# An encoder block's head: which channel blocks share a bank of the transposes, and where VectorE's second copy of weights stands

## The chip, the cores and the metric

The kernel runs on one core of a Trainium2 chip. The metric is the device time of one execution, in microseconds, as the median of several runs. Beside it there is one profiled execution, whose trace gives a start and a duration for each instruction. The engines are named as in the profile: PE is TensorE (PEld its weight loads), ACT is ScalarE, DVE is VectorE, POOL is GpSimd, SP is SyncE, which issues most of the loads.

## What is computed

One layer of an encoder block on 256 tokens of 1024 channels, in float32:

```
h  = RMSNorm(x)                       # 256 x 1024
z  = h @ W_in                         # pool-in, pool-gate, q, k, v, attn-gate, merge gates
yA = (pooled(z.pool_in) * silu(z.pool_gate)) @ W_a
yB = (dilated_attention(q, k, v) * silu(z.attn_gate)) @ W_b
y  = RMSNorm(x + (sigmoid(gA) * yA + sigmoid(gB) * yB) @ W_out)
```

The attention has three groups of eight heads with windows of different dilation, combined by their softmax denominators. The matrix products must keep nearly the accuracy of float32.

## The kernel before

**Products in three passes.** An operand a is split into a high part, a rounded to the format float32r, and a low part, the rest. A product is then three matmuls into one accumulator: high by high, high by low, low by high. For the weights the parts are called `whi` and `wlo`, for the normalised and transposed tokens `hh` and `hl`. The weights come in pieces of about 1 MB in a fixed order (`wraw0`, `wraw1`, ...), four buffers deep; ACT makes `whi` (line 128) and DVE makes `wlo` (line 133) of a piece, in halves, while PE still works on earlier pieces.

**The head.** Everything that the change touches stands in the first part of `encoder_block`, which is written under a manual schedule: ACT, DVE, PE and POOL execute it in the order of the text, and waits are set where an instruction needs another engine's result. Two engines that access one PSUM bank are given such a wait too. In order:

- PE multiplies a dummy tile while the tokens load. The tokens `X` come in two halves of 128 tokens (b = 0, 1).
- For each half, ACT and DVE sum the squares of one half of the channels each, POOL makes the reciprocal root `rs`, and DVE (line 194, channels 0 to 511) and ACT (line 195, channels 512 to 1023) scale it to `XN`.
- DVE rounds piece 0 of the weights to `whi` in two copies of 128 x 1024 (line 197), each when its half of the load has landed. POOL then makes `wlo` of it in two subtractions (lines 199 and 200, helper at line 163).
- PE transposes `XN` in sixteen steps of 128 x 128 (`turn`, line 204): eight channel blocks kc for b = 0, then for b = 1. The transposed blocks lie in four PSUM banks `tp0` to `tp3` of two blocks each. Block kc lies in bank kc % 4, so blocks 0 and 4 share a bank, 1 and 5, and so on. For b = 1 the order of the transposes is 0, 4, 1, 5, 2, 6, 3, 7, which completes one bank after the other.
- For each kc, ACT reads the block from its bank, multiplies it by the norm's gain and rounds it to `hh` (line 223); DVE reads the same block, multiplies it likewise and subtracts `hh`, which gives `hl` (line 224).
- PE multiplies the blocks with piece 0 of the weights as they come (`part0`, line 213): the pair of matmuls (for the two column blocks) with `hh` of block kc, then the pair with `hl` of block kc - 2; at the end the two last pairs with `hl`. After these 32 matmuls come 16 with `wlo` and `hh`, of which the last six, for blocks 5 to 7, need POOL's second subtraction. Before these six stand a few small matmuls for the position bias (line 237).

After the head PE goes on with piece 1 of the weights (`project_t`, lines 247 to 249 in `mm3`), and so on through all pieces, with the attention's steps in between.

Of the kernel before, what the change touches and what calls it, by code (L numbers as in the profile page):

```python
# [17 lines left out]
P = 128  # L18
# [24 lines left out]
def encoder_block(ctx: ExitStack, tc: tile.TileContext, x, w_in, lines, w_pool, w_proj_a, w_proj_b,  # L43
                  w_out, final_gain, params, out):
    nc = tc.nc
# [7 lines left out]
    def slot(shape, dt, tag, name, bufs=1):  # L53
        return sb.tile(shape, dt, tag=tag, name=name, bufs=bufs)
# [6 lines left out]
    def bank(shape, tag, name, bufs):  # L61
        return ps.tile(shape, F32, tag=tag, name=name, bufs=bufs)
# [8 lines left out]
    ident = sb.tile([P, P], F32, name="ident")  # L71
# [64 lines left out]
    def cut_next():  # L136
        cut_half()
        cut_half()
# [16 lines left out]
    XN = slot([P, 2, D], F32, "v", "XN", 2)  # L155
# [5 lines left out]
    def cut_lo(n, k0, k1, eng):  # L161
        t, (hi, lo) = raws[n][0], parts[n]
        return eng.tensor_tensor(lo[:, k0:k1, :], t[:, k0:k1, :], hi[:, k0:k1, :].bitcast(F32), op=ALU.subtract)

    def open_parts(n):
        shp = raws[n][1]
        parts[n] = (slot([P] + shp, F32R, "whi", f"whi{n}", 3), slot([P] + shp, F32R, "wlo", f"wlo{n}", 3))
        state["cut"] = 2 * n + 2

    with tc.manual_schedule(engines={mybir.EngineType.Activation, mybir.EngineType.DVE, mybir.EngineType.PE,  # L170
                                    mybir.EngineType.Pool}):
        tiny = sb.tile([P, 1], F32, name="tiny")
        warm = sb.tile([P, P], F32, name="warm")
        nc.vector.memset(warm, 0.0)
        nc.scalar.activation(tiny, warm[:, 0:1], AF.Square)

        def keep_warm(times):
            for _ in range(times):
                nc.tensor.matmul(misc[:, P:2 * P], warm, warm, start=True, stop=True)

        keep_warm(WARM)
        halves = [slice(h * 512, (h + 1) * 512) for h in range(2)]
        for b in range(2):
            sq = [slot([P, 512], F32, "st", f"sq{b}{h}", 3) for h in range(2)]
            nc.scalar.activation(sq[0], X[:, b, halves[0]], AF.Square, scale=1.0 / 32.0, accum_out=ss[:, b, 0:1])
            xb = X[:, b, halves[1]]
            nc.vector.tensor_tensor_reduce(sq[1], xb, xb, scale=1.0 / D, scalar=EPS, op0=ALU.mult, op1=ALU.add,
                                           accum_out=ss[:, b, 1:2])
            t = slot([P, 1], F32, "rt", f"rt{b}", 2)
            nc.vector.tensor_tensor(t, ss[:, b, 0:1], ss[:, b, 1:2], op=ALU.add)  # L190
            nc.gpsimd.tensor_tensor(rs[:, b:b + 1], t, mhalf, op=ALU.pow)
        open_parts(0)
        for b in range(2):
            nc.vector.tensor_scalar(XN[:, b, halves[0]], X[:, b, halves[0]], rs[:, b:b + 1], None, op0=ALU.mult)
            nc.scalar.activation(XN[:, b, halves[1]], X[:, b, halves[1]], AF.Copy, scale=rs[:, b:b + 1])
        for k in (0, 4):
            nc.vector.tensor_copy(parts[0][0][:, k:k + 4, :], raws[0][0][:, k:k + 4, :])

        cut_lo(0, 0, 5, nc.gpsimd)
        first_lo = cut_lo(0, 5, 8, nc.gpsimd)  # L200
        tps = [bank([P, 2, S], "mm" if i < 3 else "T", f"tp{i}", 3 if i < 3 else 2) for i in range(4)]

        def turn(kc, b):
            nc.tensor.transpose(tps[kc % 4][:, kc // 4, b * P:(b + 1) * P], XN[:, b, kc * P:(kc + 1) * P], ident)

        acc = bank([P, 2, 512], "S", "k00", 1)
        acc0 = [acc[:, u, 0:S] for u in range(2)]

        def part0(kc, x):
            hi_, lo_ = parts[0]  # L210
            for u in range(2):
                c = slice(u * P, (u + 1) * P)
                nc.tensor.matmul(acc0[u], (lo_ if x == 2 else hi_)[:, kc, c], (hl if x == 1 else hh)[:, kc, :],
                                 start=x == 0 and kc == 0, stop=x == 2 and kc == KC - 1)

        for kc in range(KC):
            turn(kc, 0)
        for kc in range(KC):
            turn(kc // 2 + kc % 2 * 4, 1)
        for kc in range(KC):  # L220
            v = tps[kc % 4][:, kc // 4]
            gcol = prm[:, kc:kc + 1]
            nc.scalar.activation(hh[:, kc, :], v, AF.Copy, scale=gcol)
            nc.vector.scalar_tensor_tensor(hl[:, kc, :], v, gcol, hh[:, kc, :].bitcast(F32), op0=ALU.mult,
                                           op1=ALU.subtract)
            part0(kc, 0)
            if kc >= 2:
                part0(kc - 2, 1)
        for kc in (6, 7):
            part0(kc, 1)  # L230
        for kc in range(KC):
            if kc == 5:

                for t in range(3):
                    w = 3 * NH
                    o = 3 * P + t // 2 * w
                    nc.tensor.matmul(misc[:, t * w:(t + 1) * w], oh[:, t * P:(t + 1) * P], oh[:, o:o + w],
                                     start=True, stop=True)
            part0(kc, 2)
        cut_next()  # L240
        nc.vector.tensor_copy(line.rearrange("p i r h -> p r i h"),
                              misc[:, 0:LROW * NH].rearrange("p (r i h) -> p r i h", i=2, h=4))
        cut_next()
# [270 lines left out]
    for g, w in enumerate(POOL_W):  # L514
        h = w // 2
        cur, lo_, n_ = U[:, g, :], 0, UW
        k = 1
# [305 lines left out]
```

## Time and profile before

| | us |
|---|---|
| median of 3 runs (lowest to highest) | 260.86 (260.79 to 261.13) |
| the profiled execution, its own time | 260.82 |
| its span, from the first instruction's start to the last one's end | 259.0 |
| PE busy | 250.4 |
| DVE busy | 210.2 |
| ACT busy | 164.4 |
| POOL busy | 74.5 |

In rows of the timeline the first number is the start in us from the beginning of the span, the second the duration in us. Then come the engine, the line of the code, the operation, the tiles written and read, their shapes and the count of instructions that the row holds. In brackets stands how long the engine was idle before, and what ended that. A row whose count is over 1 holds neighbours of the same kind, of which one may begin before the last has ended. Ends of matmuls are modelled, so their starts are the better measure.

### The profile page before, as it was taken

What the parts mean: (1) busy time and instruction counts of PE and PEld (TensorE: products, weight loads), DVE (VectorE), ACT (ScalarE), POOL (GpSimd) and SP (SyncE); (2) the same over time, 40 slices, a digit from 0 to 9 for tenths busy, and PEclk for the clock granted to TensorE, in tenths of its full rate; (3) what the DMA queues carried; (4) which work ended last, traced back from release to release, by engine and by line L of the source; (5) the groups of instructions that cost most, each with busy time, mean ns of one, the idle gap of its engine ahead of it and who ended that gap; (6) DMA issues with size and microseconds to landing.
All of it is one profiled execution on the core that took longest, in us unless ns stands there. A gap on an engine that the chain in (4) does not pass through costs nothing.

```text
span 259.0 us, 5482 instructions
## 1 busy us (share of the span) xinstructions
PE 250.4 (97%) x2160; PEld 248.8 (96%) x2160; DVE 210.2 (81%) x412; ACT 164.4 (63%) x285; POOL 74.5 (29%) x101
## 2 busy tenths in 40 slices
PE   7899999999999999999999999999999999999990
PEld 7899999999999999999999999999999999999990
DVE  2899988778888787889697997967859988899383
ACT  4878577565666565658967777765457797446141
POOL 1563386002798000010763910000010020442011
PEclk9999999999999999999999999999999999999998
DMA  6999999984445553444989867144440696300022
GB/s 231 393 412 363 239 323 329 313 306 162 166 162 172 235 172 156 162 164 162 284 254 257 278 216 273 47 164 162 164 162 6 209 383 233 148 4 0 0 84 81
DMA packets 9992, 52.01 MB, mean 201 GB/s; under 512 B 1147, under 2 KB 2142, under 8 KB 4718
## 3 DMA queue, kind: packets, MB, share of 16 engines
q1 hardware_dynamic: 7022, 44.08, 48.4%
q0 software_dynamic: 2512, 7.12, 11.1%
q10 hardware_dynamic: 432, 0.46, 0.5%
q8 instruction: 17, 0.28, 0.4%
q14 instruction: 9, 0.07, 0.1%
HBM read 47.42 MB, written 1.09 MB: 187 GB/s over the span
## 4 chain that ended last, share of the span: by engine, by line
PE 84%; DVE 6%; issue 3%; ACT 2%; DMA 2%; POOLq 0%; POOL 0%; SPq 0%; DVEq 0%; ACTq 0%
PE v L249 4%; PE v L248 4%; PE q L249 4%; PE q L248 4%; PE v L247 4%; PE q L247 4%; PE g L247 4%; PE g L248 4%; PE g L249 4%; PE k L247 4%; PE k L249 4%; PE k L248 4%; PE y L247 2%; PE y L248 2%; PE y L249 2%
## 5 line engine op out<-in xcount | busy, mean ns | idle before, releaser
L133 DVE TENSOR_TENSOR wlo<-wraw,whi 128x512 fp32r<-128x512 f32 (+2 forms) x134 | 108.5, 849 | 8.3 <-ACT whi L128 7.3
L128 ACT ACTIVATE whi<-wraw 128x1024 fp32r<-128x1024 f32 (+1 forms) x80 | 81.0, 1038 | 23.2 <-PE q L248 10.1
L247 PE MATMUL g<-hh,whi 128*128 128x256 f32 x128 | 35.8, 280 | 0.0
L249 PE MATMUL g<-hh,wlo 128*128 128x256 f32 x128 | 35.4, 277 | 0.0
L248 PE MATMUL g<-hl,whi 128*128 128x256 f32 x128 | 35.4, 276 | 0.0
L304 ACT ACTIVATE st<-st,nm 128x512 f32<-128x512 f32 x16 | 11.6, 722 | 29.6 <-DVE nm L301 29.6
L247 PE MATMUL v<-whi,hh 128*128 128x256 f32 x96 | 26.6, 277 | 0.0
L249 PE MATMUL v<-whi,hl 128*128 128x256 f32 x96 | 26.5, 276 | 0.0
L248 PE MATMUL v<-wlo,hh 128*128 128x256 f32 x96 | 26.5, 276 | 0.0
L249 PE MATMUL q<-hh,wlo 128*128 128x256 f32 x96 | 26.5, 276 | 0.0
L247 PE MATMUL q<-hh,whi 128*128 128x256 f32 x96 | 26.5, 276 | 0.0
L248 PE MATMUL q<-hl,whi 128*128 128x256 f32 x96 | 26.5, 276 | 0.0
L247 PEld LDWEIGHTS g<-hh,whi 128*128 128x128 f32 x128 | 24.0, 188 | 0.1
L248 PEld LDWEIGHTS g<-hl,whi 128*128 128x128 f32 x128 | 24.1, 188 | 0.0
L249 PEld LDWEIGHTS g<-hh,wlo 128*128 128x128 f32 x128 | 24.0, 188 | 0.0
L247 PE MATMUL k<-hh,whi 128*128 128x256 f32 x80 | 22.2, 277 | 0.0
L249 PE MATMUL k<-hh,wlo 128*128 128x256 f32 x80 | 22.1, 277 | 0.0
L248 PE MATMUL k<-hl,whi 128*128 128x256 f32 x80 | 22.1, 277 | 0.0
L248 PEld LDWEIGHTS v<-wlo,hh 128*128 128x128 f32 x96 | 18.0, 188 | 0.0
L249 PEld LDWEIGHTS q<-hh,wlo 128*128 128x128 f32 x96 | 18.0, 188 | 0.0
L248 PEld LDWEIGHTS q<-hl,whi 128*128 128x128 f32 x96 | 18.0, 188 | 0.0
L247 PEld LDWEIGHTS q<-hh,whi 128*128 128x128 f32 x96 | 18.0, 188 | 0.0
(177 smaller groups left out, 760.2 us busy)
## 6 DMA issues: line engine op xcount, KB each, us to landing
wraw<-in_w_in_dram SPq DMA_DIRECT2D x31, 1024.0 KB, 6.4
wraw<-in_w_out_dram SPq DMA_DIRECT2D x4, 1024.0 KB, 4.9
T<-line_d POOLq DMA_DIRECT2D x4, 576.0 KB, 6.8
KX<-KX POOLq DMA_DIRECT2D x8, 256.0 KB, 14.5
wraw<-in_w_proj_a_dram SPq DMA_DIRECT2D x2, 1024.0 KB, 4.7
wraw<-in_w_proj_b_dram SPq DMA_DIRECT2D x2, 1024.0 KB, 4.9
X<-in_x_dram SPq DMA_DIRECT2D x2, 512.0 KB, 4.2
wraw<-in_w_in_dram SPq DMA_DIRECT2D x2, 512.0 KB, 6.6
```

The source lines that it names most:

```text
L128: nc.scalar.activation(hi[:, s, :], t[:, s, :], AF.Copy)
L133: nc.vector.tensor_tensor(lo[:, s, :], t[:, s, :], hi[:, s, :].bitcast(F32), op=ALU.subtract)
L247: nc.tensor.matmul(acc, ah, bh, start=first, stop=False)
L248: nc.tensor.matmul(acc, ah, bl, start=False, stop=False)
L249: nc.tensor.matmul(acc, al, bh, start=False, stop=last)
L304: e = nc.scalar.activation(st, st, AF.Exp, bias=nm, scale=-1.0, accum_out=l)
```

## The change

Three things change in the head.

- Block kc lies in bank kc // 2 instead of kc % 4, so neighbours share a bank: 0 and 1, 2 and 3, 4 and 5, 6 and 7. For b = 1 the blocks are transposed in the order 0 to 7, which again completes one bank after the other.
- DVE's second copy of piece 0's weights stands behind `hl` of block 0 instead of in front of it.
- POOL's two subtractions for piece 0's `wlo` are written behind that copy. Their order among POOL's instructions stays the same.

All later lines of the file move by four. Behind the head, two neighbouring pairs of instructions for pieces 3 and 4 of the weights and the key blocks change places on ACT and DVE.

```diff
-        for k in (0, 4):
+        def copy0(k):
             nc.vector.tensor_copy(parts[0][0][:, k:k + 4, :], raws[0][0][:, k:k + 4, :])
 
-        cut_lo(0, 0, 5, nc.gpsimd)
-        first_lo = cut_lo(0, 5, 8, nc.gpsimd)
+        copy0(0)
         tps = [bank([P, 2, S], "mm" if i < 3 else "T", f"tp{i}", 3 if i < 3 else 2) for i in range(4)]
 
         def turn(kc, b):
-            nc.tensor.transpose(tps[kc % 4][:, kc // 4, b * P:(b + 1) * P], XN[:, b, kc * P:(kc + 1) * P], ident)
+            nc.tensor.transpose(tps[kc // 2][:, kc % 2, b * P:(b + 1) * P], XN[:, b, kc * P:(kc + 1) * P], ident)
...
         for kc in range(KC):
             turn(kc, 0)
         for kc in range(KC):
-            turn(kc // 2 + kc % 2 * 4, 1)
+            turn(kc, 1)
         for kc in range(KC):
-            v = tps[kc % 4][:, kc // 4]
+            v = tps[kc // 2][:, kc % 2]
             gcol = prm[:, kc:kc + 1]
             nc.scalar.activation(hh[:, kc, :], v, AF.Copy, scale=gcol)
             nc.vector.scalar_tensor_tensor(hl[:, kc, :], v, gcol, hh[:, kc, :].bitcast(F32), op0=ALU.mult,
                                            op1=ALU.subtract)
+            if kc == 0:
+                copy0(4)
+
+                cut_lo(0, 0, 5, nc.gpsimd)
+                first_lo = cut_lo(0, 5, 8, nc.gpsimd)
             part0(kc, 0)
             if kc >= 2:
                 part0(kc - 2, 1)
```

## The prediction

> **What bounds the kernel now.** I read the page first, then the chain of work that ended last, then the timeline of the head in narrow windows, one instruction at a time. The page says that the tensor engine (PE) is busy nearly all the time:
>
> ```profile
> span 259.0 us, 5482 instructions
> PE 250.4 (97%) x2160; PEld 248.8 (96%) x2160; DVE 210.2 (81%) x412; ACT 164.4 (63%) x285; POOL 74.5 (29%) x101
> ```
>
> The chain in the window from 5 to 17 us (start, length, what) shows that from 7.21 us on the path to the end runs through PE alone: sixteen transposes, the first channel block's matmuls, then the next block.
>
> ```profile
> 7.21 2.15 PE tp L204 x16
> 9.36 5.28 PE k L213 x42
> 14.64 0.58 PE misc L237 x6
> 15.22 0.77 PE k L213 x6
> 15.99 0.11 PE k L247
> ```
>
> The view by stages (length, then busy us of PE, PEld, DVE, ACT, POOL, the granted clock, DMA) shows no gap afterwards: 36.30 of 36.30 us, then 186.70 of 187.00. So a microsecond by which the head delays PE is a microsecond at the end, and the question is only when PE finishes the head.
>
> ```profile
> 6.00:8.00 2.00, 0.82 (x8) 0.79 (x8) 1.45 (x5) 1.53 (x4) 0.90 (x2) 1.00 0.87 317
> 26.70:63.00 36.30, 36.30 (x321) 36.30 (x320) 29.71 (x46) 24.07 (x39) 11.11 (x11) 1.00 1.01 294
> 63.00:250.00 187.00, 186.70 (x1623) 185.95 (x1622) 155.26 (x318) 119.17 (x206) 50.43 (x66) 1.00 0.50 166
> 250.00:259.00 9.00, 2.91 (x26) 2.71 (x24) 4.58 (x15) 2.15 (x7) 0.67 (x1) 0.86 0.33 117
> ```
>
> In the head, ScalarE (ACT) rounds each block kc of the transposed tokens from a PSUM bank to hh (I write hh0 to hh7), and VectorE (DVE) subtracts it from the same bank to get hl0 to hl7. In time order, one instruction a row:
>
> ```profile
> 8.74 0.47 ACT L223 ACTIVATE hh<-tp,prm 128x256 fp32r<-128x256 f32 x1 [0.42 <-PE tp L204]
> 9.12 0.47 ACT L223 ACTIVATE hh<-tp,prm 128x256 fp32r<-128x256 f32 x1
> 9.47 0.47 ACT L223 ACTIVATE hh<-tp,prm 128x256 fp32r<-128x256 f32 x1
> 9.83 0.48 ACT L223 ACTIVATE hh<-tp,prm 128x256 fp32r<-128x256 f32 x1
> 9.71 0.48 DVE L224 SCALAR_TENSOR_TENSOR hl<-tp,prm,hh 128x256 fp32r<-128x256 f32 x1
> 10.22 0.48 ACT L223 ACTIVATE hh<-tp,prm 128x256 fp32r<-128x256 f32 x1
> 10.10 0.47 DVE L224 SCALAR_TENSOR_TENSOR hl<-tp,prm,hh 128x256 fp32r<-128x256 f32 x1
> 10.61 0.47 ACT L223 ACTIVATE hh<-tp,prm 128x256 fp32r<-128x256 f32 x1
> 10.88 0.48 DVE L224 SCALAR_TENSOR_TENSOR hl<-tp,prm,hh 128x256 fp32r<-128x256 f32 x1
> 11.39 0.48 ACT L223 ACTIVATE hh<-tp,prm 128x256 fp32r<-128x256 f32 x1
> 12.45 0.48 DVE L224 SCALAR_TENSOR_TENSOR hl<-tp,prm,hh 128x256 fp32r<-128x256 f32 x1
> ```
>
> The first four hh follow each other every 0.36 us. hh4 starts at 10.22, 0.03 after hl0 ends (9.71 + 0.48); hh5 at 10.61, 0.04 after hl1; hh7 at 11.39, 0.03 after hl3. hh4 reads the bank that hl0 read, and waits for it, though both only read. Today the partner in the bank is four blocks away, so DVE's own pace (0.39) hides this wait.
>
> **The change, part by part.** On ACT, from hh0 on, each with its wait, before and after:
>
> ```order
> L223 ACTIVATE hh_85<-tp0_138,prm_73 128x256 [waits DMAHW0_49,PE_49]
> L223 ACTIVATE hh_85<-tp1_139,prm_73 128x256 [waits PE_49]
> L223 ACTIVATE hh_85<-tp2_140,prm_73 128x256 [waits PE_49]
> L223 ACTIVATE hh_85<-tp3_141,prm_73 128x256 [waits PE_49]
> L223 ACTIVATE hh_85<-tp0_138,prm_73 128x256 [waits DVE_49]
> ```
>
> ```order
> L222 ACTIVATE hh_85<-tp0_135,prm_73 128x256 [waits DMAHW0_49,PE_49]
> L222 ACTIVATE hh_85<-tp0_135,prm_73 128x256 [waits DVE_49]
> L222 ACTIVATE hh_85<-tp1_136,prm_73 128x256 [waits PE_49]
> L222 ACTIVATE hh_85<-tp1_136,prm_73 128x256 [waits DVE_49]
> L222 ACTIVATE hh_85<-tp2_137,prm_73 128x256 [waits PE_49]
> ```
>
> Four waits on DVE remain, but now every odd block waits for the block just before it. On DVE, from the copies of block 0's weights (whi) on, before and after:
>
> ```order
> L197 CAST whi0_128<-wraw0_76 128x1024 x2
> L224 SCALAR_TENSOR_TENSOR hl_86<-tp0_138,prm_73,hh_85 128x256
> L224 SCALAR_TENSOR_TENSOR hl_86<-tp1_139,prm_73,hh_85 128x256
> L224 SCALAR_TENSOR_TENSOR hl_86<-tp2_140,prm_73,hh_85 128x256
> L224 SCALAR_TENSOR_TENSOR hl_86<-tp3_141,prm_73,hh_85 128x256
> ```
>
> ```order
> L197 CAST whi0_128<-wraw0_76 128x1024
> L223 SCALAR_TENSOR_TENSOR hl_86<-tp0_135,prm_73,hh_85 128x256
> L197 CAST whi0_128<-wraw0_76 128x1024
> L223 SCALAR_TENSOR_TENSOR hl_86<-tp0_135,prm_73,hh_85 128x256
> L223 SCALAR_TENSOR_TENSOR hl_86<-tp1_136,prm_73,hh_85 128x256 x2
> ```
>
> hl0 passes the second copy. On PE, the transposes of the second token block, before and after:
>
> ```order
> L204 MATMUL tp_138<-ident,XN 128x128 [waits DVE_49]
> L204 MATMUL tp_138<-ident,XN 128x128 [waits Activation_49]
> L204 MATMUL tp_139<-ident,XN 128x128 x2
> L204 MATMUL tp_140<-ident,XN 128x128 x2
> L204 MATMUL tp_141<-ident,XN 128x128 x2
> ```
>
> ```order
> L203 MATMUL tp_135<-ident,XN 128x128 [waits DVE_49]
> L203 MATMUL tp_135<-ident,XN 128x128
> L203 MATMUL tp_136<-ident,XN 128x128 x2
> L203 MATMUL tp_137<-ident,XN 128x128 [waits Activation_49]
> L203 MATMUL tp_137<-ident,XN 128x128
> ```
>
> The second of them, the tenth in all, which frees the first bank for hh0, no longer waits for ACT. The rows for the other terms: the transposes (shortest, median and longest ns; five at their pace; the ninth and the tenth), DVE's and ACT's halves of the normalised tokens, DVE's second copy, POOL's two low parts of block 0's weights, block 1's low part on DVE, and PE's stations.
>
> ```profile
> L204 PE MATMUL tp<-ident,XN x16: 272/273/330, 7.2 to 9.1; 128*128 128x128 f32 x16
> ...
> 7.49 0.71 PE L204 MATMUL tp<-ident,XN 128*128 128x128 f32 x5
> 8.14 0.33 PE L204 MATMUL tp<-ident,XN 128*128 128x128 f32 x1
> 8.38 0.33 PE L204 MATMUL tp<-ident,XN 128*128 128x128 f32 x1
> 7.60 0.49 DVE L194 TENSOR_SCALAR XN<-X,rs 128x512 f32<-128x512 f32 x1 [0.45 <-POOL rs L191]
> 7.60 0.72 ACT L195 ACTIVATE XN<-X,rs 128x512 f32<-128x512 f32 x1 [0.47 <-POOL rs L191]
> 9.10 0.69 DVE L197 CAST whi<-wraw 128x1024 fp32r<-128x1024 f32 x1 [0.41 <-DMA wraw<-in_w_in_dram]
> 9.87 2.99 POOL L163 TENSOR_TENSOR wlo<-wraw,whi 128x1280 fp32r<-128x1280 f32 x1 [2.30 <-DVE whi L197]
> 12.79 1.87 POOL L163 TENSOR_TENSOR wlo<-wraw,whi 128x768 fp32r<-128x768 f32 x1
> 11.77 1.06 ACT L128 ACTIVATE whi<-wraw 128x1024 fp32r<-128x1024 f32 x1
> 15.65 1.21 DVE L133 TENSOR_TENSOR wlo<-wraw,whi 128x1024 fp32r<-128x1024 f32 x1
> 9.27 0.39 PE L213 MATMUL k<-hh,whi 128*128 128x256 f32 x1
> 9.49 0.53 PE L213 MATMUL k<-hh,whi 128*128 128x256 f32 x2
> 9.64 0.38 PE L213 MATMUL k<-hh,whi 128*128 128x256 f32 x1
> 13.32 1.32 PE L213 MATMUL k<-hh,wlo 128*128 128x256 f32 x10
> 15.83 0.28 PE L247 MATMUL k<-hh,whi 128*128 128x256 f32 x1
> 16.06 0.28 PE L249 MATMUL k<-hh,wlo 128*128 128x256 f32 x1
> ```
>
> Start of the chain, a small gain: the tenth transpose sat until ACT's half ended (7.60 + 0.72 = 8.32); it now needs DVE's half only (7.60 + 0.49 = 8.09). It goes 0.11 after 8.14 (the pace of the five: 0.71 less the 0.27 of one, over four), at 8.25 instead of 8.38, and ends the median 0.27 later, at 8.52. hh0 goes from 8.74 to 8.57 and ends at 9.04.
>
> Then, with 0.03 for each hand-over: hl0 9.07 to 9.55, hh1 9.58 to 10.06, hl1 10.09 to 10.57. The second copy fits between hl0 and hl1: from 9.46 (0.39 after hl0), and DVE is free 0.61 later (9.71 - 9.10) at 10.07, so it costs nothing; without that cover it would cost up to its 0.69. From here a pair of blocks takes: hl(odd) to hl(even) 0.39, hl(even) and hand-over 0.51, hh(odd) and hand-over 0.51, together 1.41 us. Before it was two DVE paces, 0.78. Three pairs on, hl7 runs from 10.09 + 4.23 = 14.32 to 14.80 (before: 12.45 to 12.93), and hh7, a hand-over and a length earlier, from 13.81 to 14.29.
>
> PE starts the pair of hh7 0.06 after it (as 9.27 after hh0's end, 9.21), at 14.35. After a wait the second matmul comes 0.22 later (9.27, 9.49) and the next 0.15 (9.64), so 14.72 for the pair of hl5. From there to the first matmul with wlo are six steps of 0.113 (36.30 us over 321), 0.68; hl7, ready for PE at 14.86, no longer stops them. So that matmul starts at 15.40, where it started at 13.32: **+2.08 us**.
>
> The rest has cover. POOL starts 0.36 later, since the copy ends at 10.15 (was 9.79): its pieces end at 13.22 and 15.01, the first wanted at 15.40, the second ten and six matmuls later. Block 1's whi starts 0.38 after hh7, at 14.19, and ends at 15.25; wlo1's halves take 1.21 each, at most to 17.7, and PE wants them at 16.06 + 2.08 = 18.14 and twelve matmuls later. So nothing behind the head comes late. Further down a later wlo piece goes ahead of a key block's low part on DVE; it takes no engine time more, and PE's queue is unchanged there.
>
> The profiled execution took 260.82 us, span and 1.82 around it; the median of the runs is 260.86. Forecast: 260.82 + 2.08 = 262.90.
>
> Bounds: a hand-over could cost ACT-to-PE's 0.06; nine lie in the chain, +0.3, and the copy's full length adds 0.1: +2.5. If PE is released by hl7 alone (14.86 + 0.22 + 0.15 = 15.23), +1.9. Later short waits of PE (0.30 us in the longest stage above) could take up 0.3: +1.6. With the runs' spread of 0.3 (260.79 to 261.13) at the wider end, and half of it below, 262.2 to 263.6.
>
> **Rivals.**
> (a) Not slower: the shared bank doesn't bind. Then hh1 follows hh0 at 0.36, DVE alone sets the pace: hl1 at 10.07, hl7 at 10.07 + 6 x 0.39 = 12.41, against 12.45 before. That gives about 260.8; at the very best PE's waiting goes (13.32 - 9.27 is 4.05 us for 32 matmuls of 0.113, so 0.4) and 0.2 of earlier start, 260.2. For it: the hl0 term and the tenth transpose do gain. Against it: three rows in which ACT starts 0.03 after DVE's read of its bank. It decides below a pair time of about 0.80 us, where hl7 would be no later than now; the rows give 1.41. [...] Chance 0.07.
>
> (b) More: PE's clock falls, since PE now works some 0.9 of each 1.41 us between 9 and 14.3. If half the clock were granted for as long as that stretch, 5.2 us, the matmuls of an equal time would take 2.6 us more: 265.5. For it: the clock mean is 0.86 in the last 9 us, with PE busy 2.91. Against: it is 1.00 in 6 to 8 us, with PE busy 0.82 of 2.00. [...] Chance 0.05.
>
> **Chances.** The forecast has 0.88. A measurement of this kernel tells about 0.2% (0.5 us) from no change; the forecast and (b) lie beyond it, (a) mostly within: faster 0.02, same 0.05, slower 0.93. The range leaves out both rivals.
>
> **What would show it.** Right: hh1, hh3, hh5, hh7 each start 0.03 after the hl before them; hl7 ends near 14.8; the first wlo matmul starts near 15.4; all later stages moved by the same 2 us, at clock 1.00. Wrong: hh1 starts before hl0 ends (a); the matmul pace of 0.11 doubles after 12 us (b); the head is 2 us late but the end is not, in which case something off PE had slack that no row here shows.

## The result, and the profile after

| | before | after |
|---|---|---|
| median of 6 runs (lowest to highest), us | 260.88 (260.79 to 261.13) | 262.91 (262.37 to 263.00) |
| profiled execution, its own time, us | 260.82 | 262.88 |
| its span, us | 259.0 | 261.1 |

The changed kernel is slower: the ratio after to before is 1.0073, with a 95% interval of 1.0061 to 1.0085. From one profiled execution to the other it is 262.88 - 260.82 = 2.06 us. Among the runs of the experiments below, two executions took far longer than all others and are left out of the ratios: one of the kernel before (282.5 us), and one of the kernel with the move of `hl` alone (1432 us), which was the profiled one.

The chain that ended last, of the changed kernel, from the transposes on (start, length, what):

```profile
7.27 1.38 PE tp L203 x10
8.65 0.02 issue
8.68 0.48 ACT hh L222
9.16 0.03 issue
9.18 0.48 DVE hl L223
9.67 0.60 DVE whi L197
10.27 0.83 DVE hl L223 x2
11.10 0.02 issue
11.12 0.48 ACT hh L222
11.60 0.03 issue
11.63 0.89 DVE hl L223 x2
12.51 0.02 issue
...
13.96 0.48 ACT hh L222
14.44 0.04 issue
14.48 2.32 PE k L212 x18
```

Before, this stretch of the chain was PE alone. Now it goes to and fro between ACT and DVE, with an odd hh, the hl of the same block and the next even hl in each round (in the first round the second copy of the weights stands in the place of hh1), and comes back to PE at 14.48 only. The round repeats every 1.42 us: 9.70, 11.12, 12.54 and 13.96 for hh1, hh3, hh5 and hh7. In the timeline of ACT the first row is hh0. Each row behind it starts with an odd block, and shows the wait in front of it:

```profile
8.68 0.47 ACT L222 ACTIVATE hh<-tp,prm 128x256 fp32r<-128x256 f32 x1 [0.29 <-PE tp L203]
9.70 0.84 ACT L222 ACTIVATE hh<-tp,prm 128x256 fp32r<-128x256 f32 x2 [0.55 <-DVE hl L223]
11.12 0.84 ACT L222 ACTIVATE hh<-tp,prm 128x256 fp32r<-128x256 f32 x2 [0.57 <-DVE hl L223]
12.54 0.84 ACT L222 ACTIVATE hh<-tp,prm 128x256 fp32r<-128x256 f32 x2 [0.58 <-DVE hl L223]
13.96 0.47 ACT L222 ACTIVATE hh<-tp,prm 128x256 fp32r<-128x256 f32 x1 [0.58 <-DVE hl L223]
```

DVE waits about as long for ACT, in the same rounds; hl0 (9.18 to 9.66) is followed by hh1 at 9.70, 0.04 later:

```profile
9.18 0.48 DVE L223 SCALAR_TENSOR_TENSOR hl<-tp,prm,hh 128x256 fp32r<-128x256 f32 x1 [0.44 <-ACT hh L222]
9.58 0.68 DVE L197 CAST whi<-wraw 128x1024 fp32r<-128x1024 f32 x1
10.21 0.88 DVE L223 SCALAR_TENSOR_TENSOR hl<-tp,prm,hh 128x256 fp32r<-128x256 f32 x2
...
14.46 0.48 DVE L223 SCALAR_TENSOR_TENSOR hl<-tp,prm,hh 128x256 fp32r<-128x256 f32 x1 [0.54 <-ACT hh L222]
15.41 1.23 DVE L133 TENSOR_TENSOR wlo<-wraw,whi 128x1024 fp32r<-128x1024 f32 x1 [0.47 <-ACT whi L128]
```

On PE the first matmul with wlo starts at 15.50 (13.32 before), and the first one of the q projection, a later piece of the weights, at 28.87 (26.71 before):

```profile
15.50 1.18 PE L212 MATMUL k<-hh,wlo 128*128 128x256 f32 x9
28.87 0.28 PE L251 MATMUL q<-hh,whi 128*128 128x256 f32 x1
```

In the view by stages PE is then busy as before, with the clock at 1.00:

```profile
26.70:63.00 36.30, 36.30 (x322) 36.30 (x321) 28.14 (x46) 22.65 (x39) 10.48 (x13) 1.00 1.01 278
63.00:250.00 187.00, 186.70 (x1623) 185.94 (x1623) 155.92 (x315) 120.37 (x207) 49.81 (x65) 1.00 0.51 171
```

So nearly the whole delay of the head reaches the end: 2.16 us at the q projection, 2.06 us in the total.

### The profile page after: what moved, and what is told of

Read it like the earlier page. It is cut to its first block, busy times and chain, and to the rows that moved or that the text cites. A ratio compares the mean times of both kernels' runs of the same rounds, so it can differ in the third digit from the quotient of the medians.

```text
span 261.1 us, 5482 instructions
## 1 busy us (share of the span) xinstructions
PE 251.9 (96%) x2160; PEld 249.7 (96%) x2160; DVE 208.4 (80%) x412; ACT 164.6 (63%) x285; POOL 72.6 (28%) x101
## 4 chain that ended last, share of the span: by engine, by line
PE 82%; DVE 8%; issue 3%; ACT 3%; DMA 2%; POOLq 0%; POOL 0%; SPq 0%; DVEq 0%; ACTq 0%
PE v L253 4%; PE q L252 4%; PE v L252 4%; PE v L251 4%; PE q L253 4%; PE q L251 4%; PE g L251 4%; PE g L253 4%; PE g L252 4%; PE k L252 4%; PE k L251 3%; PE k L253 3%; PE y L251 2%; PE y L252 2%; PE y L253 2%
## 5 line engine op out<-in xcount | busy, mean ns | idle before, releaser
L133 DVE TENSOR_TENSOR wlo<-wraw,whi 128x512 fp32r<-128x512 f32 (+2 forms) x134 | 106.4, 834 | 10.1 <-ACT whi L128 9.3
```

The source lines that it names most:

```text
L133: nc.vector.tensor_tensor(lo[:, s, :], t[:, s, :], hi[:, s, :].bitcast(F32), op=ALU.subtract)
```

## The experiments

The theory: a read by ACT waits, as the program sets it, for DVE's read of the same bank, so what counts is how soon the bank's partner follows. Rivals: the copy moved behind hl0, with POOL's later start, carries the 2 us; or the layout itself costs, whatever the order of the blocks. Ratios are to runs of the kernel before on the same chip, with the 95% interval in brackets.

**1. Each part of the change alone.** First only the banks:

```diff
-            nc.tensor.transpose(tps[kc % 4][:, kc // 4, ...
+            nc.tensor.transpose(tps[kc // 2][:, kc % 2, ...
-            turn(kc // 2 + kc % 2 * 4, 1)
+            turn(kc, 1)
-            v = tps[kc % 4][:, kc // 4]
+            v = tps[kc // 2][:, kc % 2]
```

> Only the banks of neighbours (kc // 2, second half transposed in the order 0 to 7); both copies of weights stay in front of hl0. Theory (ACT waits for DVE's read of the shared bank, pair time 1.41 us): hl0 starts behind the copies at 9.71 instead of 9.1 to 9.2, hh1 at 10.22, hl1 at 10.73, then three pairs of 1.41, hl7 from 14.96, first wlo matmul near 16.0: 263.5 us, so about 0.6 more than the change as a whole. Rival (the 2 us come from the copy between hl0 and hl1 and from POOL's later start, not from the banks): 260.9 us, as before.

Measured: 263.46 us, ratio 1.0108 (1.0093 to 1.0123). ACT and DVE of this kernel (the second copy, hl0, hl1 with hl2, hl7):

```profile
10.19 0.84 ACT L223 ACTIVATE hh<-tp,prm 128x256 fp32r<-128x256 f32 x2 [1.05 <-DVE hl L224]
```

```profile
9.07 0.69 DVE L197 CAST whi<-wraw 128x1024 fp32r<-128x1024 f32 x1 [0.36 <-DMA wraw<-in_w_in_dram]
9.68 0.48 DVE L224 SCALAR_TENSOR_TENSOR hl<-tp,prm,hh 128x256 fp32r<-128x256 f32 x1
10.70 0.88 DVE L224 SCALAR_TENSOR_TENSOR hl<-tp,prm,hh 128x256 fp32r<-128x256 f32 x2 [0.54 <-ACT hh L223]
...
14.96 0.48 DVE L224 SCALAR_TENSOR_TENSOR hl<-tp,prm,hh 128x256 fp32r<-128x256 f32 x1 [0.54 <-ACT hh L223]
```

All stations are within 0.03 us of where the theory had them (10.22, 10.73, 14.96), and the first matmul with wlo is at 15.99. The banks alone cost more than the whole change, and the first rival falls: under shared banks, hl0's move gains about 0.5 us (hl7 at 14.96 here, 14.46 in the whole change).

Then only the move of hl0 in front of the second copy, with POOL's subtractions behind it, and the banks as before:

> Only the move of hl0 in front of the second copy, with POOL's work behind it; banks kc % 4 as before. Theory: the hl follow each other every 0.39 us, hl7 0.14 later than before; POOL starts after the copy, about 0.5 later than before, and its parts now land at about the moment PE wants them (13.4 and 15.2 against 13.32 and 15.07): 260.9 to 261.1 us, 0 to 0.2 more than before. Rival (the copy and POOL carry the 2 us): 262.9 us, as the whole change.

Measured: 261.49 us, ratio 1.0032 (1.0019 to 1.0045), more than the 0 to 0.2 us of the theory and far from the rival's 2. The rows of this kernel are read from a second run of it, in number 4.

**2. Neighbours in a bank, but not neighbours in time.** The whole change, with the blocks taken in another order by ACT, DVE and PE:

```diff
-        for kc in range(KC):
+        seq = (0, 2, 4, 6, 1, 3, 5, 7)
+        for i, kc in enumerate(seq):
...
-            if kc >= 2:
-                part0(kc - 2, 1)
-        for kc in (6, 7):
+            if i >= 2:
+                part0(seq[i - 2], 1)
+        for kc in seq[6:]:
```

> The whole change, but the blocks are taken in the order 0, 2, 4, 6, 1, 3, 5, 7 by ACT, DVE and PE, so neighbours still share a bank, and the two reads of a bank by ACT are four blocks apart in time. Theory (what counts is how soon the partner in the bank follows): hh1 no longer waits for the copy and hl0 in a row, the hl go every 0.39, hl7's place ends near 12.9; PE waits for the second copy of weights one pair earlier (block 4 is third), about 0.2: 261.0 to 261.1 us. Rival (the layout or the copy costs the 2 us, whatever the order of the blocks): 262.9 us.

Measured: 261.65 us, ratio 1.0049 (1.0031 to 1.0066). The seven hl after the copy now run through without a wait, 2.83 us for all of them. So by the medians half of the 2 us is gone with the same banks and the same copy, but 0.6 more is left than I worked out. (Two of the nine runs took 263.0 us, the others 261.1 to 261.8. The two raise the ratio, and no trace shows why they were longer.) The rows of DVE, POOL and PE show where:

```profile
10.19 2.83 DVE L224 SCALAR_TENSOR_TENSOR hl<-tp,prm,hh 128x256 fp32r<-128x256 f32 x7
13.26 2.85 POOL L163 TENSOR_TENSOR wlo<-wraw,whi 128x768 fp32r<-128x768 f32 x1
13.08 1.35 DVE L133 TENSOR_TENSOR wlo<-wraw,whi 128x1024 fp32r<-128x1024 f32 x1
15.09 0.74 PE L242 MATMUL misc<-oh 99*128 99x24 f32 x6
16.17 0.50 PE L212 MATMUL k<-hh,wlo 128*128 128x256 f32 x2 [0.33 <-POOL wlo L163]
```

POOL's second part took 2.85 us instead of 1.87, and PE waited for it: the last six wlo matmuls follow the small ones at 16.17, 1.08 after these began, where it was 15.07 - 14.48 = 0.59 before. DVE's subtraction for the next piece had begun at 13.08, ahead of POOL's second part. (In this kernel and in those of number 4, the build also puts one or two matmuls of the next piece in front of PE's last pair with hl; that is work moved and not added.)

**3. Partners two apart.** The kernel before, with blocks 0 and 2, 1 and 3, 4 and 6, 5 and 7 in a bank:

```diff
-            nc.tensor.transpose(tps[kc % 4][:, kc // 4, ...
+            nc.tensor.transpose(tps[kc % 2 + kc // 4 * 2][:, kc // 2 % 2, ...
-        for kc in range(KC):
-            turn(kc // 2 + kc % 2 * 4, 1)
+        for kc in (0, 2, 1, 3, 4, 6, 5, 7):
+            turn(kc, 1)
-            v = tps[kc % 4][:, kc // 4]
+            v = tps[kc % 2 + kc // 4 * 2][:, kc // 2 % 2]
```

> The kernel before with blocks 0 and 2, 1 and 3, 4 and 6, 5 and 7 in a bank: partners two apart, copies in front. Theory: hh2 waits for hl0 and hl2 for hh2, but hl1 runs meanwhile; worked through with 0.48 a read, 0.03 a hand-over and 0.39 between two hl, hl7 starts at 12.91 against 12.45: first wlo matmul 0.35 to 0.5 later, 261.2 to 261.4 us, between partners four apart (260.9) and next to each other (263.5 with the copies in front). Rival (banks without effect): 260.9 us or a little less, since hh0's bank is complete 0.13 earlier.

Measured: 261.49 us, ratio 1.0029 (1.0018 to 1.0041), a little above the upper end. The rows of DVE show pairs and quadruples of hl, with the small gaps of this distance between them (9.79 to 10.66, then 10.81). The rows of ACT and PE show where the time went:

```profile
10.30 1.60 ACT L223 ACTIVATE hh<-tp,prm 128x256 fp32r<-128x256 f32 x4 [0.80 <-DVE hl L224]
10.83 0.51 PE L213 MATMUL k<-hh,whi 128*128 128x256 f32 x2 [0.78 <-ACT hh L223]
9.79 0.87 DVE L224 SCALAR_TENSOR_TENSOR hl<-tp,prm,hh 128x256 fp32r<-128x256 f32 x2
10.81 1.66 DVE L224 SCALAR_TENSOR_TENSOR hl<-tp,prm,hh 128x256 fp32r<-128x256 f32 x4
12.62 0.88 DVE L224 SCALAR_TENSOR_TENSOR hl<-tp,prm,hh 128x256 fp32r<-128x256 f32 x2
```

The first matmul with wlo came at 14.13, 0.81 later than before, where I had worked out 0.35 to 0.5 from hl7. It was not hl7 that delayed PE: hh2 had to wait for hl0, which ends at 10.27, PE stood 0.78 us until hh2 was there, and from 10.83 on it ran without a stop. So the mechanism, the wait for the partner's read, is the one expected, but it costs at the start of the blocks and not at their end.

With the copies in front, then, partners four apart are the kernel before, two apart cost 0.29%, and next to each other 1.08%.

**4. Where the move of hl0 loses time on its own.** The kernel with the move alone again:

> The move of hl0 alone once more, for its trace. The even-first kernel lost 0.5 us more than worked out, since DVE's first piece of wlo1 began at 13.08, ahead of POOL's second part, which then took 2.85 us instead of 1.87 and ended at 16.1. Theory: the same happens here; DVE's hl7 ends near 13.1, POOL's first part near 13.4, so DVE's wlo1 is first, POOL's second part ends near 16.0, and the last six wlo matmuls start near 16.1 instead of 15.07: 261.4 to 261.8 us. Rival (PE late because of the hl themselves): POOL's second part takes 1.9, the first wlo matmul is at 13.7 or later, and no gap stands between the small matmuls and the last six.

Measured: 261.61 us, ratio 1.0032 (1.0020 to 1.0043). Its rows agree with the theory:

```profile
13.35 2.81 POOL L163 TENSOR_TENSOR wlo<-wraw,whi 128x768 fp32r<-128x768 f32 x1
13.02 1.46 DVE L133 TENSOR_TENSOR wlo<-wraw,whi 128x1024 fp32r<-128x1024 f32 x1
14.78 0.75 PE L241 MATMUL misc<-oh 99*128 99x24 f32 x6
16.21 0.50 PE L212 MATMUL k<-hh,wlo 128*128 128x256 f32 x2 [0.69 <-POOL wlo L163]
```

The six last matmuls with wlo did not start before 16.21. The test is to take POOL's second part off POOL, and put it on DVE in front of the subtraction that had overtaken it:

```diff
-                cut_lo(0, 0, 5, nc.gpsimd)
-                first_lo = cut_lo(0, 5, 8, nc.gpsimd)
+                first_lo = cut_lo(0, 0, 5, nc.gpsimd)
...
+        cut_lo(0, 5, 8, nc.vector)
         for kc in range(KC):
             if kc == 5:
```

> The move of hl0 alone, with the second part of block 0's wlo (blocks 5 to 7) subtracted by DVE right behind hl7, in place of POOL. Theory (what the move costs is POOL's part pushed behind DVE's): DVE waits for POOL's first part (13.4), its part of 768 takes about 0.9 and lands at 14.3, in time for 15.1; what is left is the first part, 0.1 late: 260.7 to 260.9 us, against 261.4 to 261.8 with POOL's second part. Rival (the hl or the copy cost it): still 261.4 to 261.8 us.

Measured: 260.39 us, ratio 0.9992 (0.9983 to 1.0000).

```profile
10.50 2.97 POOL L163 TENSOR_TENSOR wlo<-wraw,whi 128x1280 fp32r<-128x1280 f32 x1 [2.85 <-DVE whi L197]
13.08 1.21 DVE L163 TENSOR_TENSOR wlo<-wraw,whi 128x768 fp32r<-128x768 f32 x1
14.97 0.74 PE L241 MATMUL misc<-oh 99*128 99x24 f32 x6
15.56 0.93 PE L212 MATMUL k<-hh,wlo 128*128 128x256 f32 x6
```

The wait of the six matmuls is gone, and with it nearly the whole loss of the move (0.19 us are left by the table behind number 5). The same edit on the even-first kernel of number 2:

> The whole change in the order 0, 2, 4, 6, 1, 3, 5, 7, with the second part of block 0's wlo on DVE. Theory: without POOL's late part what is left of the even-first kernel is the first wlo matmul at 13.7 to 13.9 instead of 13.3: 261.0 to 261.2 us, so 1.8 us of the change are gone by the order of the blocks and the part on DVE, with the banks still shared by neighbours. Rival (the shared banks cost by themselves): 261.6 us as before the move to DVE, or more.

Measured: 260.65 us, ratio 1.0007 (0.9998 to 1.0017), even less than I had worked out. Both parts of the change are in this kernel, and nearly all of the 2 us is gone, so neither the shared bank nor the copy costs that much by itself. The 0.29 us that the table behind number 5 still shows go with a wait of PE for the second copy, since the third block in this order, block 4, is the first that needs it:

```profile
10.31 0.48 PE L212 MATMUL k<-hh,whi 128*128 128x256 f32 x2 [0.35 <-DVE whi L197]
```

**5. The shared banks, in the even-first order, with the copies in front.** Number 1's first kernel with the order of number 2:

> Neighbours share a bank, blocks in the order 0, 2, 4, 6, 1, 3, 5, 7, both copies in front of the first hl as in the kernel before, POOL's parts unchanged. Theory: hl as in the kernel before (from 9.7, every 0.39), hh0 0.13 earlier, the first wlo matmul 13.2 to 13.3; POOL's second part begins at 12.79 and DVE's wlo1 at 12.87, so POOL stays first: 260.6 to 260.9 us, the same as before within 0.2%. Rival (the shared banks cost by themselves): 261.5 us or more. If DVE wins the race by these 0.08 us: 261.4 us.

Measured: 260.50 us, ratio 0.9994 (0.9985 to 1.0002): no change. POOL's second part stayed ahead of DVE's subtraction (12.81 against 12.87), and its two parts end at 14.66 as in the kernel before. When neighbours share a bank and the copies stand in front, the order of the blocks alone moves the ratio from 1.0108 to 0.9994, about 3 us. No kernel here beats the one before by more than the measurement tells.

**All kernels by one station.** The totals also hold a difference of pace late in the kernel, described at the end. The start of the first matmul of the q projection doesn't. Counted from DVE's first row of `XN`, so that the moment at which the tokens landed drops out, the profiled executions give:

| kernel | `XN` on DVE | first matmul of q | later than before |
|---|---|---|---|
| before | 6.68 | 26.71 | |
| whole change | 6.73 | 28.87 | 2.11 |
| banks only (1) | 6.70 | 29.36 | 2.63 |
| whole change, even blocks first (2) | 6.74 | 27.75 | 0.98 |
| partners two apart (3) | 6.72 | 27.50 | 0.75 |
| move of hl0 alone (4) | 6.69 | 27.65 | 0.93 |
| the same, second part on DVE (4) | 6.76 | 26.98 | 0.19 |
| even first, second part on DVE (4) | 6.63 | 26.95 | 0.29 |
| even first, copies in front (5) | 6.69 | 26.71 | -0.01 |

The last three came out below the totals expected of them, while by this station they lose 0.19, 0.29 and nothing. Their traces have the quicker of the two paces and that of the kernel before the slower, so the rest was not gained by the edits as far as the rows show.

## Why the prediction was right

- **The pair time.** Predicted 1.41 us from 0.39 + 0.51 + 0.51; measured 1.42. The rows of ACT, the distance series (four, two, one apart) and the two orders of the blocks show that the wait for the partner's read makes it.
- **The start of the chain.** hh0 was to start at 8.57 and started at 8.68 (before: 8.74); hl0 9.07, measured 9.18; hl1 10.09, measured 10.21. Some 0.06 us of this 0.11 is the tokens, whose load ended later in this execution, so that PE's first transpose started at 7.27 instead of 7.21. The rest is the tenth transpose: I had put it 0.11 us after the ninth, the pace of transposes that follow each other, but it started at 8.37, 0.17 after the ninth's 8.20. The ninth had waited for DVE, and after such a wait the second transpose came 0.17 later in the kernel before too (7.21, 7.38).
- **The copy between hl0 and hl1.** Predicted to fit, and it did: DVE's row of hl1 follows the copy without a wait, at the time when hh1 ends (9.70 + 0.47 = 10.17). It is covered narrowly: hl1 starts 0.63 us after the copy's start, and where the next hl had no hh to wait for (numbers 2 and 4) it started 0.59 to 0.60 after it.
- **PE.** The first wlo matmul was worked out at 15.40, 2.08 late; it came at 15.50, 2.18 late, and the q projection 28.87 - 26.71 = 2.16 late. At the end 2.06 us were left; 0.12 of the difference is taken up between the first matmul of the tile `pt` (68.31 before, 70.47 after) and that of the tile `a` (71.94 and 73.98). So the mechanism and its size were right, but that the total of 262.90 meets 262.88 so closely is luck: an error of 0.1 in the head, 0.06 of it the later tokens, and 0.1 taken up later cancel.
- **POOL.** Its parts were to end at 13.22 and 15.01, ahead of need; in the trace they ended at 13.29 and 15.09 and did not hold PE up, which wanted them at 15.50 and 17.23. This reason was right for the change as a whole, and hid something: DVE's subtraction comes at 15.41 there, after POOL is through, because the pairs hold DVE back. Without the pairs, DVE arrives at 13.0, overtakes POOL's second part, and PE loses time on it (number 4). My expectations for the move alone and for the even-first kernel had taken POOL's duration as fixed, and failed in that term.
- **Rivals.** (a), that the bank does not bind, is refuted by ACT's rows; (b), the clock, by the 1.00 in the stages above and in every 2 us from 6 to 16, where PE is busy 1.46 to 1.79 of 2.00 us; in the last stage, behind 250 us, it is 0.87, where it was 0.86 before. Half the clock, from which the 265.5 of (b) was worked out, is granted in neither trace while PE has work: in the kernel before it is 0.76 from 256 to 257 us and 0.50 behind, and PE's last matmul starts at 252.63; in the changed one it is 0.64 from 258 to 259 and 0.50 behind. The longest wait of PE among the pairs is 0.53 us.

## What to carry to other kernels

Where a program lets one engine's read of a PSUM bank wait for another's, as this one does, lay out the blocks so that those which share a bank are far apart in the order of work: here, with the copies in front, four apart was free (the eight hl of the kernel before ran without a wait, 3.22 us in all), two cost 0.3% and neighbours 1.1%. Reordering the work did as well here as moving the blocks (ratio 0.9994 in number 5). And before an operation moves, look at which operation it lets overtake one of another engine, since a part that is covered by its queue place today may not be tomorrow (here POOL's second part, 1.87 us before and 2.81 to 2.85 once DVE's subtraction came first).

## What the runs showed of the hardware

**DVE and POOL subtractions ran one after the other, and the order of arrival decided.** The row of POOL's 128 x 768 part is 1.87 us in the kernel before, where DVE's subtraction came after it and took 2.86 instead of 1.21; it is 2.85 and 2.81 where DVE's came first. The later of the two ends about its own length after the earlier: in the kernel before DVE's at 15.73, 1.07 us after POOL's, and in the move alone POOL's at 16.16, 1.68 us after DVE's. In number 4, DVE's 128 x 768 part took 1.21 us from 13.08, where I had expected 0.9; POOL's first part ran to 13.47, and DVE's ended 0.82 later. The row of DVE in the kernel before, beside POOL's part from 12.79 to 14.66, and DVE's next row in the move alone, beside POOL's part from 13.35 to 16.16:

```profile
12.87 2.86 DVE L133 TENSOR_TENSOR wlo<-wraw,whi 128x1024 fp32r<-128x1024 f32 x1
```

```profile
14.40 2.83 DVE L133 TENSOR_TENSOR wlo<-wraw,whi 128x1024 fp32r<-128x1024 f32 x1
```

The hl, with one input from PSUM, went on every 0.39 beside POOL's first part. What keeps the subtractions apart, no trace here shows; the rows show 2.86 against 1.21 us on DVE, and 2.81 to 2.85 against 1.87 on POOL.

**The same matmuls ran at two paces.** In a stage of the output projections (matmul durations in ns: shortest, median, longest), the kernel before and the one of number 4 with the move alone and DVE's part:

```profile
L247 PE MATMUL y<-ATHL,whi x29: 281/281/281, 219.0 to 228.9; 128*128 128x256 f32 x29
```

```profile
L251 PE MATMUL y<-ATHL,whi x30: 276/276/387, 218.8 to 228.8; 128*128 128x256 f32 x30
```

In the windows from 207.5 to 229 us they hold 182 and 187 matmuls in 21.36 busy us each, both at clock 1.00. From the first matmul of `y` to the first of the tile behind it, `both`, three of the nine traces take 22.93 or 22.94 us (before, the whole change, the move alone), the other six 22.39 to 22.45. That is about 0.5 us of the total. It did not enter the result, as both profiled executions went at the slower pace. There is one trace of each kernel, so that one kernel changes its pace from execution to execution is not shown. The times fit it: runs of the kernel before spread from 260.1 to 261.0 on the chips of the experiments, and the kernel of number 1 with the banks alone, whose trace has the quicker pace, took 262.85 us in that execution and 263.42 to 263.64 in its three others. What sets the pace is open. Differences under 0.5 us are therefore better read from the starts of instructions in the head than from two totals.

**Left open.** ACT's wait for DVE's read is one that the program sets (the waits on DVE in the prediction's rows). Whether ACT could read the bank while DVE does was not tried.
